# First input projection of a two-layer trunk: both conditioning products first, the filter's last layer behind the first tiles, the second token half normed in one piece

## The chip, the cores and the metric

One core of a Trainium2 chip. The metric is the device time of one execution in microseconds (us). Engines are named as in the profile: PE (TensorE matmul, PEld its weight loads), DVE (VectorE), ACT (ScalarE), POOL (GpSimd), SP (SyncE, which issues most loads). Each engine works through its own queue in order.

## The reference, cut to what matters

A two-layer trunk for 512 latent and 128 context tokens, width 1024. Layer 0 mixes an mLSTM and a Hyena long convolution behind one input projection, layer 1 is attention; each layer ends with a gated ConvFFN. What the change touches is the norm ahead of a sub-layer, its modulation from the conditioning vectors, and the filters of the long convolution:

```python
def adaln(cvec, w, b):
    mod = jax.nn.silu(cvec) @ w + b
    return jnp.split(mod[:, None, :], 6, axis=-1)
hp = rmsnorm(xp, g_mix[l]) * (1.0 + sc_p1) + sh_p1      # context
hs = rmsnorm(xs, g_mix[l]) * (1.0 + sc_s1) + sh_s1      # latents
proj = h @ w_in
# hyena_filters: two sine layers, then
filt = hdn @ w3
filt = filt * jnp.exp(-t * deltas)
# long_conv_bidir: K = rfft([h_past, 0, reversed h_future]); y = irfft(rfft(u) * K)
```

## The kernel before

The 640 tokens lie in the free dimension, features in the 128 partitions (8 blocks k of 1024). They are worked in two halves a of 320; the second half holds 192 latent and 128 context tokens, which have different shifts and scales. Every weight tile and activation is split in a high and a low fp32r part (`wh`, `wl`; `XH`, `XL`), and a product is three matmuls of 320 columns per k and half. `split_w` (L99 to L104) makes `wh` on ACT and `wl` on the engine it is given.

`norm_part` (L302 to L328) makes `XH` and `XL` of one k: for each range of tokens with one modulation a multiply on DVE (L321), a shift and cast on ACT (L325) and a subtraction on DVE (L326). The first half is one range, the second half two. One norm (`keep`, ahead of the last ConvFFN) has a form for the second half that takes the 320 tokens at once: a multiply by the row factor (L308), two scale-and-shift steps on ACT in place (L311), a cast on ACT (L313), a subtraction on DVE (L314). `norm_part` serves four norms: ahead of the input projection (n0), the first ConvFFN (n1), the attention (n2) and the last ConvFFN (n3, with `keep`).

`mixer_ab` (from L754) begins the program. In the order in which its instructions are written: the loads of the filter's tables and of x; the row factors of both halves (`rms`); the second step of the generator `hyena_filters` (the load of `w3`, the two sine layers on PE, ACT and DVE, sum and difference of `w3` on POOL, their split `wA` and `wB`, and five Exp steps `ad`); then `ada_pe` for feature half 0 (8 loads `wa` of 512 KB, 32 matmul records on PE, a copy `adasb` on ACT, 8 small matmuls `adaq`, then `mod` and `coefA` on DVE); the third filter step (20 matmuls `ff`, ten multiplies into `ad`, six steps for a boundary row on POOL); the norm of k 0 to 3; the first two projection tiles `hya0`, `hya1` with `wl` on POOL; `ada_pe` for half 1 with 8 more loads `wa`, which use the same 8 buffers again; the norm of k 4 to 7. Then `linear` runs the tiles `hya0` to `hya3`; the first two are a pair that takes k 0 to 3 of both halves and then k 4 to 7. After the pair the filter's last step follows (spectra: 28 matmul records `fa`, `fb`, `fp` of 512 columns, and DVE steps into `Ksp`, `Kpp`), then `hyena_chunk` and the tiles `hyb`.

PSUM has two pairs of banks (`pmt`) and four single banks (`pst`). Projection tiles and `ff` take pairs; `rms` holds two singles until the norm is done; `ada_pe` and the spectra take singles. A planner puts the instructions into each engine's queue: by and large as written, with later ones moved ahead where it reckons that the earlier ones must wait. So the queues of the trace are not strictly the written order.

Of the kernel before, what the change touches and what calls it, by code (L numbers as in the profile page):

```python
# [16 lines left out]
P = 128  # L17
# [5 lines left out]
HT = T // 2  # L23
# [13 lines left out]
def trunk(ctx: ExitStack, tc: tile.TileContext, I, O, dbg=None, stop=None):  # L37
# [19 lines left out]
    def pmt(nm):  # L57
        return psum["m"].tile([P, 2, 512], F32, tag="pm", name=nm)
# [40 lines left out]
    def split_w(raw, n, nm, eng):  # L99
        wh = wp.tile([P, 1024], F32R, tag="wh", name=f"{nm}h")  # L100
        wl = wp.tile([P, 1024], F32R, tag="wl", name=f"{nm}l")
        act.copy(out=wh[:, :n], in_=raw[:, :n])
        eng.tensor_tensor(out=wl[:, :n], in0=raw[:, :n], in1=wh[:, :n].bitcast(F32), op=ALU.subtract)  # L103
        return wh, wl  # L104

# [196 lines left out]
    def norm_part(l, which, nrm, a, rb, ks, keep=None):  # L302
        n = 2 * l + which
        for k in ks:
            if keep and a:
                t = keep[2 + k // 4][:, k % 4]
                c = slice(HT, T)
                dve.tensor_tensor(out=t, in0=x[:, k, c], in1=rb[:, :HT], op=ALU.mult)  # L308
                for c0, c1, s in RANGES[1]:
                    u = t[:, c0 - HT : c1 - HT]  # L310
                    act.activation(out=u, in_=u, func=AF.Identity, scale=coefA[:, n, k, s : s + 1],  # L311
                                   bias=mod[:, l, 3 * which, k, s : s + 1])
                act.copy(out=XH[:, k, c], in_=t)  # L313
                last = dve.tensor_tensor(out=XL[:, k, c], in0=t, in1=XH[:, k, c].bitcast(F32), op=ALU.subtract)  # L314
                continue
            for c0, c1, s in RANGES[a]:
                if keep:
                    t = keep[2 * a + k // 4][:, k % 4, c0 - a * HT : c1 - a * HT]
                else:
                    t = nrm.tile([P, HT], F32, tag="nt", name=f"nt{n}{k}_{c0}", bufs=4 if n == 0 else 6)[:, : c1 - c0]  # L320
                dve.scalar_tensor_tensor(out=t, in0=x[:, k, c0:c1], scalar=coefA[:, n, k, s : s + 1],  # L321
                                         in1=rb[:, c0 - a * HT : c1 - a * HT], op0=ALU.mult, op1=ALU.mult)
                b = mod[:, l, 3 * which, k, s : s + 1]
                oh, ol = XH[:, k, c0:c1], XL[:, k, c0:c1]
                act.activation(out=oh, in_=t, func=AF.Identity, bias=b)  # L325
                last = dve.scalar_tensor_tensor(out=ol, in0=t, scalar=b, in1=oh.bitcast(F32), op0=ALU.add,  # L326
                                                op1=ALU.subtract)
        return last.ins  # L328
# [320 lines left out]
    def hyena_filters(fl, spectra):  # L649
# [13 lines left out]
        for t_, n_ in ((z, "k_z"), (w1, "w_f1"), (fb, "f_cols"), (w2, "w_f2")):  # L663
            sp.dma_start(out=t_, in_=I[n_])
        yield
        w3 = load_raw(I["w_f3"], "fw3")
        for t_, n_ in ((delta, "k_delta"), (tneg, "k_tneg")):
            sp.dma_start(out=t_, in_=I[n_])

        ad = fl.tile([P, 2, 5, 512], F32, name="ad")  # L670
        frb = fl.tile([64, 2], F32, name="frb")
        for j in range(2):
            dve.tensor_tensor(out=frb[:, j : j + 1], in0=fb[:, 0:1], in1=fb[:, 1 + j : 2 + j], op=ALU.mult)
# [1 line left out]
        for j, w in enumerate((w1, w2)):  # L675
            pp = pmt(f"fm{j}")
            pt = [pp[:, 0], pp[:, 1]]
            pe.matmul(pt[0][0:64, :], w, hid[:, 0:512], start=True, stop=True)
            pe.matmul(pt[1][0:64, 0:128], w, hid[:, 512:640], start=True, stop=True)
            arg = arg_[j]  # L680
            for (c0, c1, a) in ((0, 512, 0), (512, 640, 1)):
                act.activation(out=arg[:, c0:c1], in_=pt[a][0:64, : c1 - c0], func=AF.Identity,
                               scale=fb[:, 0:1], bias=frb[:, j : j + 1])
            MAGIC = 12582912.0
            dve.tensor_scalar(out=kk, in0=arg, scalar1=1.0 / (2 * math.pi), scalar2=MAGIC, op0=ALU.mult, op1=ALU.add)
            dve.tensor_scalar(out=kk, in0=kk, scalar1=MAGIC, scalar2=None, op0=ALU.subtract)
            c1_ = 6.28125
            c2_ = float(np.float32(2 * math.pi - c1_))
            dve.scalar_tensor_tensor(out=arg, in0=kk, scalar=-c1_, in1=arg, op0=ALU.mult, op1=ALU.add)
            dve.scalar_tensor_tensor(out=arg, in0=kk, scalar=-c2_, in1=arg, op0=ALU.mult, op1=ALU.add)  # L690
            lim = 3.14159250
            dve.tensor_scalar(out=arg, in0=arg, scalar1=lim, scalar2=-lim, op0=ALU.min, op1=ALU.max)
            act.activation(out=hid[0:64, :], in_=arg, func=AF.Sin)
            if j == 0:

                for c, op in enumerate((ALU.add, ALU.subtract)):
                    pool.tensor_tensor(out=ws[:, c], in0=w3[:, 0:512], in1=w3[:, 512:], op=op)
                act.copy(out=wA, in_=ws)
                dve.tensor_tensor(out=wB[0:64], in0=ws[0:64], in1=wA[0:64].bitcast(F32), op=ALU.subtract)
                pool.memset(wB[64:].bitcast(F32), 0.0)  # L700

        hs = fl.tile([P, 640], F32R, tag="kk", name="hs", bufs=1)
        act.copy(out=hs[0:64], in_=hid[0:64])
        dve.tensor_tensor(out=hs[64:], in0=hid[0:64], in1=hs[0:64].bitcast(F32), op=ALU.subtract)
        for r in range(5):
            act.activation(out=ad[:, 0, r], in_=delta, func=AF.Exp, scale=tneg[:, r : r + 1])
        yield
        for r in range(5):
            pp = pmt(f"ff{r}")
            pt = [pp[:, 0], pp[:, 1]]  # L710
            lh = hs[:, r:512:4] if r < 4 else hs[:, 512:640]
            for j in range(2):
                pe.matmul(pt[j], lh, wA[:, j], start=True, stop=False)
                pe.matmul(pt[j], lh, wB[:, j], start=False, stop=True)
            for j in (1, 0):
                dve.tensor_tensor(out=ad[:, j, r], in0=pt[j], in1=ad[:, 0, r], op=ALU.mult)
            if r in (0, 4):

                row = fl.tile([64, 640], F32, tag="arg", name=f"row{r}", bufs=1)[0:1, 0:512]
                pool.tensor_tensor(out=row, in0=ad[0:1, 0, r], in1=ad[0:1, 1, r], op=ALU.add)  # L720
                for j in range(2):
                    pool.tensor_scalar(out=ad[0:1, j, r], in0=row, scalar1=0.5, scalar2=None, op0=ALU.mult)
        yield
        Ksp, Kpp, tabs = spectra
        for t_, n_ in ((tabs, "k_tabs"), (neg, "k_neg")):
# [28 lines left out]
    def mixer_ab():  # L754
        with ExitStack() as es:
# [29 lines left out]
            with ExitStack() as en:  # L785
                fl = en.enter_context(tc.tile_pool(name="fl", bufs=1, reuse_waits="tile"))
                nrm = en.enter_context(tc.tile_pool(name="nrm0", bufs=2, reuse_waits="tile"))
                sptr = []
                filt = hyena_filters(fl, sptr)
                es_a = en.enter_context(ExitStack())  # L790
                a0 = es_a.enter_context(tc.tile_pool(name="a0", bufs=1, side="right", reuse_waits="tile"))
                next(filt)
                for a in range(2):
                    c = slice(a * HT, (a + 1) * HT)
                    sp.dma_start(out=x[:, :, c], in_=I["x"][:, :, c])
                rbs = [rms(f"n0{a}", a, nrm) for a in range(2)]
                for t_, n_ in ((cwh, "w_conv_hy"), (cwq, "w_conv_qk")):
                    pool.dma_start(out=t_, in_=I[n_])
                next(filt)
                for half in range(2):  # L800
                    for _ in ada_pe(0, ((0, half), (1, half)), a0, "adr", 8):
                        pass
                    if half == 0:
                        next(filt)
                    for a in range(2):
                        norm_part(0, 0, nrm, a, rbs[a], range(4 * half, 4 * half + 4))
                    if half == 0:
                        pre = [load_w(w_, f"hya{j}", eng=pool) for j, w_ in enumerate(W(0, 1))]
                es_a.close()
                hy = es_h.enter_context(tc.tile_pool(name="hy", bufs=1, side="right", reuse_waits="tile"))  # L810
                tabs = hy.tile([P, 5, 2, P], F32, name="tabs")
                itab = hy.tile([P, 5, 2, P], F32, name="itab")
                Ksp = hy.tile([P, 4, 2, 4, P], F32, name="Ksp")
                Kpp = hy.tile([P, 4, 2, P], F32, name="Kpp")
                sptr.extend((Ksp, Kpp, tabs))
                linear(W(0, 1, 2, 3), done_h, "hya", filler=lambda: next(filt, 0), kcut=4, pre=pre, x_last=True)
                sp.dma_start(out=itab, in_=I["k_itab"])
# [819 lines left out]
```

## Time and profile before

| | |
|---|---|
| three runs | 1698.2, 1694.92, 1697.67 us |
| median | 1697.67 us |
| the profiled execution | 1698.56 us, span 1696.8 us |
| busy share of the span | PE 97%, DVE 69%, ACT 43%, POOL 8% |
| granted TensorE clock, mean | 0.993 of full speed |

The page gives busy times over the whole span. The change is made in the first 60 us and in three norms, so the stretches of the span have to be read one by one. A busy PE is not PE at its peak: matmul durations overlap, and a new matmul can start before the one before it is shown as ended. Start times tell the pace.

### The profile page before, as it was taken

The page shows a single profiled execution, that of the slowest core. Times are in us where ns is not written, and L with a number is a line of the kernel's source. Part 1 is how long each engine was busy: PE and PEld are TensorE (multiplying, and loading weights), DVE is VectorE, ACT ScalarE, POOL GpSimd, SP SyncE. Part 2 cuts the span into 40 slices and gives each one's busy share as a digit, 9 for nine tenths or more (in the row PEclk, how much of TensorE's full clock was granted, in tenths as well). Part 3 has the DMA queues.
Part 4 walks back from the last instruction along what each step waited for, and adds up shares of the span by engine and source line. Part 5 has one row for each costly group of instructions (what it writes and reads, how often), then busy time and mean ns, then how long its engine had stood idle before and what let it go on. Part 6 is the DMA issues. An engine that isn't in the chain of part 4 may idle for free. (4 is left out here: it accounts for less than half of the span.)

```text
span 1696.8 us, 28240 instructions
## 1 busy us (share of the span) xinstructions
PE 1642.3 (97%) x11206; PEld 1561.0 (92%) x11206; DVE 1179.1 (69%) x2361; ACT 735.2 (43%) x1380; POOL 135.0 (8%) x152
## 2 busy tenths in 40 slices
PE   5999999999999999999998999999999999999996
PEld 2699888999999999999998898889999999999996
DVE  5887556675887677777458555556388679587785
ACT  6333346663433123213336555656276335244353
POOL 3110001001000000000011212121010000000001
PEclk9999999999999999999999999999999999999998
DMA  8345422142364454454222211211224222222321
GB/s 332 109 125 173 162 75 69 53 142 75 98 179 150 146 157 148 145 181 139 66 77 98 69 57 61 62 48 42 63 61 112 75 82 87 82 75 72 91 81 69
DMA packets 59092, 177.60 MB, mean 105 GB/s; under 512 B 7808, under 2 KB 15792, under 8 KB 58704
## 3 DMA queue, kind: packets, MB, share of 16 engines
q1 hardware_dynamic: 57952, 173.66, 33.0%
q0 software_dynamic: 1008, 2.13, 0.7%
q8 instruction: 88, 1.44, 0.4%
q14 instruction: 44, 0.36, 0.1%
HBM read 169.61 MB, written 4.20 MB: 102 GB/s over the span
## 5 line engine op out<-in xcount | busy, mean ns | idle before, releaser
L350 DVE SCALAR_TENSOR_TENSOR x<-pd,mod,x 128x320 f32<-128x320 f32 (+2 forms) x168 | 64.1, 434 | 126.3 <-PE pd L127 120.4
L252 DVE CUSTOM_DVE_ANT_0 adj<-adw,cb 128x1024 f32<-128x1024 f32 x112 | 136.8, 1221 | 1.6
L372 DVE SCALAR_TENSOR_TENSOR fcb<-pu,cwf,fcb 128x384 f32<-128x384 f32 (+1 forms) x100 | 54.1, 549 | 1.9
L417 DVE TENSOR_TENSOR pr<-pu,ge 128x384 f32<-128x384 f32 (+1 forms) x42 | 18.8, 486 | 50.1 <-PE pu L127 49.2
L1334 DVE CUSTOM_DVE_ANT_0 s<-pS,bm 128x384 f32<-128x384 f32 x64 | 34.3, 553 | 26.7 <-PE pS L1333 26.0
L1236 DVE TENSOR_SCALAR s<-s,nm 128x384 f32<-128x384 f32 (+1 forms) x80 | 46.2, 584 | 1.7
L1234 ACT ACTIVATE s<-s,nm 128x384 f32<-128x384 f32 x64 | 39.1, 612 | 14.1 <-DVE nm L1334 12.3
L325 ACT ACTIVATE XH<-nt,mod 128x192 fp32r<-128x192 f32 (+1 forms) x72 | 29.7, 467 | 35.7 <-DVE nt L321 35.6
L1348 ACT COPY pTs<-pS 128x384 f32<-128x384 f32 (+1 forms) x80 | 33.8, 435 | 22.4 <-PE pS L1346 21.8
L1346 PE MATMUL pS<-ident,s 128*128 128x128 f32 x208 | 36.3, 281 | 5.5 <-DVE s L1236 5.5
L278 ACT ACTIVATE sqn<-x 128x320 f32<-128x320 f32 x56 | 25.3, 465 | 36.9 <-DVE x L350 32.9
L350 DVE SCALAR_TENSOR_TENSOR x<-pop,mod,x 128x320 f32<-128x320 f32 (+2 forms) x36 | 14.3, 433 | 36.6 <-PE pop L127 26.0
L103 POOL TENSOR_TENSOR qk00l<-qk,qk00h 128x1024 fp32r<-128x1024 f32 x1 | 2.8, 2766 | 461.6 <-DVE rn L293 461.6
L407 ACT ACTIVATE ge<-fcb 128x641 f32<-128x641 f32 x22 | 16.3, 742 | 52.0 <-DVE fcb L372 52.0
L1408 POOL TENSOR_TENSOR fo<-fo,rs 128x320 f32<-128x320 f32 x8 | 6.6, 858 | 395.7 <-ACT rs L1400 395.7
L326 DVE SCALAR_TENSOR_TENSOR XL<-nt,mod,XH 128x192 fp32r<-128x192 f32 (+1 forms) x72 | 35.0, 524 | 4.2 <-ACT XH L325 4.1
L615 DVE SCALAR_TENSOR_TENSOR fcb<-fca,cwf,fcb 128x641 f32<-128x641 f32 x38 | 33.6, 884 | 3.5 <-ACT fcb L613 3.2
L1308 POOL TENSOR_TENSOR bm<-amask,wr 128x768 f32<-128x768 f32 x14 | 25.7, 1838 | 117.6 <-issue 85.9
L1346 PEld LDWEIGHTS pS<-ident,s 128*128 128x128 f32 x208 | 23.5, 141 | 11.2 <-DVE s L1236 9.5
L279 DVE TENSOR_TENSOR accn<-accn,sqn 128x320 f32<-128x320 f32 x56 | 28.9, 522 | 7.0 <-ACT sqn L278 6.1
L127 PE MATMUL pd<-G,d_0h 128*128 128x320 f32 x176 | 33.2, 309 | 0.0
L127 PE MATMUL pd<-G,d_1h 128*128 128x320 f32 x176 | 33.1, 309 | 0.0
(2133 smaller groups left out, 5860.5 us busy)
## 6 DMA issues: line engine op xcount, KB each, us to landing
adw<-in_w_adaT SPq DMA_DIRECT2D x56, 512.0 KB, 3.7
u<-in_w_up SPq DMA_DIRECT2D x50, 512.0 KB, 3.6
wa<-in_w_ada SPq DMA_DIRECT2D x40, 512.0 KB, 5.0
qk<-in_w_qkv SPq DMA_DIRECT2D x24, 512.0 KB, 3.6
d<-in_w_down SPq DMA_DIRECT2D x16, 448.0 KB, 3.4
d<-in_w_down SPq DMA_DIRECT2D x16, 384.0 KB, 3.1
d<-in_w_down SPq DMA_DIRECT2D x16, 320.0 KB, 2.9
qk<-in_w_ab SPq DMA_DIRECT2D x8, 512.0 KB, 3.6
```

The lines of the kernel that those rows point to most:

```text
L127: pe.matmul(bank(pt, a)[:, : sp_[a][1] - sp_[a][0]], ww[:, kt], xx[:, slice(*sp_[a])], start=(first and n == 0), stop=(last and n == 2))
L252: dve.tensor_tensor_reduce(out=jk, in0=w, in1=cb[:, s], op0=ALU.mult, op1=ALU.add, scale=1.0, scalar=0.0, accum_out=acc[:, k, s : s + 1])
L325: act.activation(out=oh, in_=t, func=AF.Identity, bias=b)
L326: last = dve.scalar_tensor_tensor(out=ol, in0=t, scalar=b, in1=oh.bitcast(F32), op0=ALU.add, op1=ALU.subtract)
L350: r = dve.scalar_tensor_tensor(out=x[:, k, c0:c1], in0=bank(pt, h)[:, c0 - h * HT : c1 - h * HT], scalar=mod[:, l, ch, k, s : s + 1], in1= ...
L372: dve.scalar_tensor_tensor(out=o, in0=i, scalar=w[j], in1=o, op0=ALU.mult, op1=ALU.add)
L615: dve.scalar_tensor_tensor(out=o, in0=av[:, d : d + T + 1], scalar=w[j], in1=o, op0=ALU.mult, op1=ALU.add)
L1234: act.activation(out=s, in_=src, func=AF.Exp, scale=-1.0, bias=nm, accum_out=sm)
L1236: dve.tensor_scalar(out=s, in0=s, scalar1=sm, scalar2=None, op0=ALU.mult)
L1334: dve.tensor_tensor_reduce(out=s, in0=pS[:, 0:384], in1=bm[e][:, (0, 1, 1, 2)[i]], op0=ALU.add, op1=ALU.min, scale=1.0, scalar=3.0e38, acc ...
L1346: pe.transpose(pS[:, j * P : (j + 1) * P], s[:, j * P : (j + 1) * P], ident)
L1348: act.copy(out=t[:, : nk * P], in_=pS[:, : nk * P])
```

## The change

- `ada_pe` for both feature halves comes ahead of all norms; between them the first two projection tiles are loaded and split.
- For these two tiles `wl` is no longer subtracted on POOL: ACT writes minus `wh` into `wl`, and a DMA of POOL's queue adds the raw weights to it.
- The filter generator is cut in other places. Its second step ends with the sine layers. The load of `w3` and of the decay tables, sum and difference (now on DVE), `wA`, `wB`, the Exp steps and `ff` for r = 0, 1 come behind the first pair of tiles; `ff` for r = 2 to 4 behind the tile `hya2`; the spectra behind `hya3`. `ff` takes single banks. The boundary row is made on DVE.
- In `norm_part` the second half is normed at once in all norms, as it was with `keep`.

```diff
@@ split_w
+        if eng is None:
+            act.activation(out=wl[:, :n], in_=wh[:, :n].bitcast(F32), func=AF.Copy, scale=-1.0)
+            pool.dma_start(out=wl[:, :n], in_=raw[:, :n], accum_op=ALU.add)
+            return wh, wl
@@ norm_part
-            if keep and a:
-                t = keep[2 + k // 4][:, k % 4]
+            if a:
+                if keep:
+                    t = keep[2 + k // 4][:, k % 4]
+                else:
+                    t = nrm.tile([P, HT], F32, tag="nt", name=f"nt{n}{k}_w", bufs=4 if n == 0 else 6)
@@ hyena_filters
-        w3 = load_raw(I["w_f3"], "fw3")
...
-            if j == 0:
...
-                    pool.tensor_tensor(out=ws[:, c], in0=w3[:, 0:512], in1=w3[:, 512:], op=op)
...
         dve.tensor_tensor(out=hs[64:], in0=hid[0:64], in1=hs[0:64].bitcast(F32), op=ALU.subtract)
+        yield
+        w3 = load_raw(I["w_f3"], "fw3")
...
+        for c, op in enumerate((ALU.add, ALU.subtract)):
+            dve.tensor_tensor(out=ws[:, c], in0=w3[:, 0:512], in1=w3[:, 512:], op=op)
+        act.copy(out=wA, in_=ws)
+        dve.tensor_tensor(out=wB[0:64], in0=ws[0:64], in1=wA[0:64].bitcast(F32), op=ALU.subtract)
+        pool.memset(wB[64:].bitcast(F32), 0.0)
         for r in range(5):
             act.activation(out=ad[:, 0, r], in_=delta, func=AF.Exp, scale=tneg[:, r : r + 1])
-        yield
         for r in range(5):
-            pp = pmt(f"ff{r}")
-            pt = [pp[:, 0], pp[:, 1]]
+            if r == 2:
+                yield
+                yield
+            pt = [pst(f"ff{r}{j}") for j in range(2)]
...
-                pool.tensor_tensor(out=row, in0=ad[0:1, 0, r], in1=ad[0:1, 1, r], op=ALU.add)
+                dve.tensor_tensor(out=row, in0=ad[0:1, 0, r], in1=ad[0:1, 1, r], op=ALU.add)
@@ mixer_ab
-                for half in range(2):
+                def cond_half(half):
                     for _ in ada_pe(0, ((0, half), (1, half)), a0, "adr", 8):
                         pass
-                    if half == 0:
-                        next(filt)
+
+                cond_half(0)
+                pre = [load_w(w_, f"hya{j}", eng=None) for j, w_ in enumerate(W(0, 1))]
+                cond_half(1)
+                for half in range(2):
                     for a in range(2):
                         norm_part(0, 0, nrm, a, rbs[a], range(4 * half, 4 * half + 4))
-                    if half == 0:
-                        pre = [load_w(w_, f"hya{j}", eng=pool) for j, w_ in enumerate(W(0, 1))]
```

## Rows read from the trace of the kernel before

**Rows 1.** Stretches: from:to length, busy us (instructions) per engine, PE clock, DMA share, GB/s.
```profile
0.00:50.00 50.00, 31.30 (x118) 15.76 (x121) 28.79 (x62) 28.14 (x44) 17.18 (x28) 0.93 0.76 282
```
**Rows 2.** Timeline of SP's queue: start, duration, what is issued, how many.
```profile
4.74 2.10 SPq L96 DMA_DIRECT2D fw<-in_w_f  x1
...
7.93 8.30 SPq L220 DMA_DIRECT2D wa<-in_w_ada  x8
16.75 1.61 SPq L108 DMA_DIRECT2D hya<-in_w_ab  x2
28.05 5.68 SPq L220 DMA_DIRECT2D wa<-in_w_ada  x8
```
**Rows 3.** Stretches of 5 us, columns as in group 1.
```profile
20.00:25.00 5.00, 1.82 (x8) 1.65 (x8) 4.01 (x12) 4.97 (x9) 0.00 (x0) 1.00 1.03 410
25.00:30.00 5.00, 5.00 (x28) 1.95 (x27) 3.60 (x12) 4.91 (x7) 0.00 (x0) 1.00 0.53 197
...
35.00:40.00 5.00, 4.92 (x17) 4.02 (x18) 1.89 (x6) 2.77 (x4) 3.10 (x2) 0.61 1.02 415
```
**Rows 4.** Timeline of PE and DVE: start, duration, engine, line, out<-in, how many.
```profile
35.08 0.62 PE L713 MATMUL ff<-fwA,hs 128*128 128x512 f32 x1 [1.83 <-DVE hs L704]
...
48.78 0.41 PE L118 MATMUL phya<-XH,hya0h 128*128 128x320 f32 x1
...
54.10 1.06 PE L224 MATMUL ada<-wa,csil 128*32 128x512 f32 x6
...
58.42 0.16 DVE L208 SCALAR_TENSOR_TENSOR coefA<-mod,gains 128x8 f32<-128x8 f32 x1
...
93.47 0.63 PE L845 MATMUL ut<-ident,x 128*128 128x128 f32 x4
```
**Rows 5.** The stretch from the first tile to L845, columns as in group 1.
```profile
48.70:93.30 44.60, 44.60 (x245) 34.72 (x242) 36.71 (x81) 16.81 (x35) 4.34 (x3) 1.00 0.43 139
```
**Rows 6.** PE timeline, two pairs of spectra matmuls in a row.
```profile
73.38 1.02 PE L730 MATMUL fa<-ad,tabs 128*128 128x512 f32 x2
74.24 1.02 PE L731 MATMUL fa<-ad,tabs 128*128 128x512 f32 x2
```
**Rows 7.** Groups by shape: line, engine, operation, tile, count, busy us, mean ns.
```profile
L326 DVE SCALAR_TENSOR_TENSOR XL<-nt,mod,XH 128x192 fp32r<-128x192 f32 x24 | 10.0, 417 | 2.3 <-ACT XH L325 2.3
L321 DVE SCALAR_TENSOR_TENSOR nt<-x,coefA,rbn 128x192 f32<-128x192 f32 x24 | 9.8, 408 | 2.3 <-PE rbn L299 2.3
...
L326 DVE SCALAR_TENSOR_TENSOR XL<-nt,mod,XH 128x128 fp32r<-128x128 f32 x24 | 8.3, 345 | 1.6 <-ACT XH L325 1.6
L321 DVE SCALAR_TENSOR_TENSOR nt<-x,coefA,rbn 128x128 f32<-128x128 f32 x24 | 8.2, 341 | 0.0
```
**Rows 8.** Timeline, norm n3: the last step of two k in a row, second half.
```profile
1260.97 0.49 DVE L314 TENSOR_TENSOR XL<-keep,XH 128x320 fp32r<-128x320 f32 x1 [0.70 <-ACT XH L313]
...
1262.16 0.49 DVE L314 TENSOR_TENSOR XL<-keep,XH 128x320 fp32r<-128x320 f32 x1 [0.69 <-ACT XH L313]
```
**Rows 9.** PE's waits, 820 to 1000 us (n2): total us, times, longest.
```profile
PE pqk L121 <- DVE XL L326: 1.9, 3, 1.0
```
**Rows 10.** Timelines near 415 and 418 us: three L326 without and with POOL at work.
```profile
415.17 1.53 DVE L326 SCALAR_TENSOR_TENSOR XL<-nt,mod,XH 128x320 fp32r<-128x320 f32 x3
...
418.29 2.39 POOL L103 TENSOR_TENSOR u_2l<-u,u_2h 128x1024 fp32r<-128x1024 f32 x1 [2.86 <-ACT u_2h L102]
418.71 3.25 DVE L326 SCALAR_TENSOR_TENSOR XL<-nt,mod,XH 128x320 fp32r<-128x320 f32 x3 [0.30 <-ACT XH L325]
```
**Rows 11.** DMA issues: accumulating DMAs, count, KB each, us from issue to landing.
```profile
TT<-keep POOLq DMA_DIRECT2D x2, 640.0 KB, 5.6
```
**Rows 12.** Tile ff, its DVE step: count, ns min/median/max, first and last start.
```profile
L716 DVE TENSOR_TENSOR ad<-ff,ad x10: 681/688/693, 36.6 to 49.0; 128x512 f32<-128x512 f32 x10
```
**Rows 13.** Timeline, DVE: one weight split, the four steps of one conv3.
```profile
83.03 1.22 DVE L103 TENSOR_TENSOR hya3l<-hya,hya3h 128x1024 fp32r<-128x1024 f32 x1
...
88.56 2.31 DVE L372 SCALAR_TENSOR_TENSOR abc<-phya,cwh,abc 128x384 f32<-128x384 f32 x4
```

More of the change, by code (lines that the diff above doesn't have):

```diff
@@ L665, in hyena_filters @@
         yield
-        w3 = load_raw(I["w_f3"], "fw3")
-        for t_, n_ in ((delta, "k_delta"), (tneg, "k_tneg")):
-            sp.dma_start(out=t_, in_=I[n_])
-        ad = fl.tile([P, 2, 5, 512], F32, name="ad")
         frb = fl.tile([64, 2], F32, name="frb")
@@ L693, in hyena_filters @@
             act.activation(out=hid[0:64, :], in_=arg, func=AF.Sin)
-            if j == 0:
-                for c, op in enumerate((ALU.add, ALU.subtract)):
-                    pool.tensor_tensor(out=ws[:, c], in0=w3[:, 0:512], in1=w3[:, 512:], op=op)
-                act.copy(out=wA, in_=ws)
-                dve.tensor_tensor(out=wB[0:64], in0=ws[0:64], in1=wA[0:64].bitcast(F32), op=ALU.subtract)
-                pool.memset(wB[64:].bitcast(F32), 0.0)
         hs = fl.tile([P, 640], F32R, tag="kk", name="hs", bufs=1)
@@ L704, in hyena_filters @@
         dve.tensor_tensor(out=hs[64:], in0=hid[0:64], in1=hs[0:64].bitcast(F32), op=ALU.subtract)
+        yield
+        w3 = load_raw(I["w_f3"], "fw3")
+        for t_, n_ in ((delta, "k_delta"), (tneg, "k_tneg")):
+            sp.dma_start(out=t_, in_=I[n_])
+        ad = fl.tile([P, 2, 5, 512], F32, name="ad")
+        for c, op in enumerate((ALU.add, ALU.subtract)):
[3 more added lines that the diff above has]
+        pool.memset(wB[64:].bitcast(F32), 0.0)
         for r in range(5):
             act.activation(out=ad[:, 0, r], in_=delta, func=AF.Exp, scale=tneg[:, r : r + 1])
-        yield
         for r in range(5):
-            pp = pmt(f"ff{r}")
-            pt = [pp[:, 0], pp[:, 1]]
+            if r == 2:
+                yield
+                yield
+            pt = [pst(f"ff{r}{j}") for j in range(2)]
             lh = hs[:, r:512:4] if r < 4 else hs[:, 512:640]
@@ L719, in hyena_filters @@
                 row = fl.tile([64, 640], F32, tag="arg", name=f"row{r}", bufs=1)[0:1, 0:512]
-                pool.tensor_tensor(out=row, in0=ad[0:1, 0, r], in1=ad[0:1, 1, r], op=ALU.add)
+                dve.tensor_tensor(out=row, in0=ad[0:1, 0, r], in1=ad[0:1, 1, r], op=ALU.add)
                 for j in range(2):
-                    pool.tensor_scalar(out=ad[0:1, j, r], in0=row, scalar1=0.5, scalar2=None, op0=ALU.mult)
+                    dve.tensor_scalar(out=ad[0:1, j, r], in0=row, scalar1=0.5, scalar2=None, op0=ALU.mult)
         yield
```

## The prediction, made before the changed kernel ran

> **What bounds the kernel now.** I read the stretches of the span first. In the first 50 us PE is busy for 31.3 us [rows 1]; from 48.7 to 93.3 us it is busy in all 44.6 us [rows 5]. So TensorE is the bound from about 49 us on, and whatever it starts earlier there is worth its full length at the end, as long as the others keep up. Next the loads: from 20 to 25 us they run at 410 GB/s, from 25 to 30 us at 197, from 35 to 40 us at 415 [rows 3]. SP's queue shows why there is a hole: the second eight `wa` are issued from 28.05 us on [rows 2], since they use the buffers of the first eight. Then the order on PE: `ff` begins at 35.08 us, the first tile only at 48.78, and the last group of conditioning matmuls lies among the tiles at 54.10 [rows 4]. The granted clock is 0.61 of full speed from 35 to 40 us [rows 3], a mean over 1.2 and 2.4 GHz. `ff` holds the two PSUM pairs that the first tiles need, and each `ff` step waits for its DVE multiply; that, and `coefA` of half 1 at 58.42 [rows 4], is what the first tiles wait for.
>
> **The time of the conditioning products after the change.** `w3` and the decay table (0.77 MB) leave the queue ahead of `wa` [rows 2]: 0.77 / 0.41 = 1.9 us earlier. Before, eight `wa` (4.2 MB) at 0.41 MB per us from 28.05 us with an estimated 1.5 us until data flows again (the hole in [rows 3]) end at 39.8. Without `wB` (1.2 us, by width from [rows 13]) and without the DVE time that a POOL subtraction takes (1.7 us in [rows 10]) ahead of the row factors, PE reaches the first conditioning matmuls some 3 us earlier, so the hole of 25 to 30 us, worth 5 x (1 - 197/410) = 2.6 us, can close. That gives 35.3 us. Against it stand the two accumulating DMAs. One of 640 KB took 5.6 us [rows 11], so 512 KB take some 4.5; between nothing (they fall into a hole) and 5 us for both (all engines theirs) is added to the loads: 35.3 to 40.3 us. I take 38, the middle. The Trainium skill (DMA: Bandwidth & Descriptors, Issuing engines are not separate DMA queues) says that transfers started by any engine run on the same 16 DMA engines and interleave; this speaks against the change, and by it alone one would take the upper end, 40.3 us, and a gain 2.3 us smaller. The accumulating DMAs are issued on POOL, where nothing else is queued then. From the last conditioning matmul to `coefA` it took 58.58 - 54.10 = 4.5 us [rows 4]; with 0.3 us for that matmul to start, and 4 instead of 4.5 as DVE has less in line, `coefA` of half 1 stands at 42.3 us.
>
> **The norm.** In the first half a k costs two DVE steps of 0.51 us [rows 10], about 1.0. In the second half four DVE steps of 0.41, 0.34, 0.42, 0.35 us, together 1.51 [rows 7], become two; the form for all 320 tokens ran at one k in 1.19 us, paced by ACT's three steps [rows 8]. So k 4 to 7 need 4 x 1.0 + 4 x 1.19 = 8.8 us and end at 51.1. The norm of k 0 to 3 needs half 0 alone and is done by then. Ahead of its waits PE can run k 0 to 3 of the pair (48 matmuls), so the pair ends 0.4 us (only the last k left) to 3.5 us (all of k 4 to 7 of the second tile left) after the norm: 52.5 us.
>
> In n1 and n2 the same edit saves DVE 0.3 us or more per k, but no PE wait there hangs on the second half: the 1.9 us of n2 [rows 9] are waits in its first half, where DVE stands behind POOL. The pair or trio of tiles needs 9 matmuls per k, 1.3 us, longer than 1.19. ACT's extra step costs nothing as long as this cover holds; without it, 8 x 0.4 us at the worst in each norm. I take 0, with -1 and +2 as bounds for both.
>
> **TensorE up to L845.** Before, L845 starts at 93.47 [rows 4]. Spectra: two matmul records in 0.86 us [rows 6], 28 of them 12.0 us. The 44.6 us of [rows 5] less 12.0 and some 4 of conditioning leave 28.6 for 192 tile matmuls, 0.149 each. After the pair there remain `hya2` and `hya3` (96 matmuls, 14.3 us), the spectra (12.0) and `ff` (20 of 512 columns, by width 0.24 each, 4.8): 52.5 + 31.1 = 83.6 us, 9.9 us earlier than before. `ff` is only moved; its cover before was the wait for the loads.
>
> **What the gain runs into.** DVE gets work late that it did early or POOL did. After the norm it has, up to L845: three weight splits of 1.22 and three conv3 of 2.31 [rows 13], one product of 640 columns, 0.9 by width from [rows 12], ten `ad` steps of 0.69 [rows 12], `ws` and `wB` (2.6, by width from the same rows), the boundary row (six steps on one partition, never seen on DVE: 0.15 to 0.7 each by small steps and [rows 12]; I take 0.5, as they are short in partitions, not in columns) and 14 spectra steps of 0.68: 3.7 + 6.9 + 0.9 + 6.9 + 2.6 + 3.0 + 9.5 = 33.5 us, from 51.1 to 84.6. PE wants it by 83.6. So both engines are full for 32 us, with no slack between them. Not all of it will mesh: `ff` and the spectra share four single banks that DVE empties. I count 3 us of PE waits (1 from the two ends, up to 5 from the banks). What goes away with POOL helps: three DVE steps of 0.51 took 3.25 us together while POOL ran a subtraction [rows 10]. ACT moves five Exp steps of 512 columns and a table load behind the norm, an estimated 5 us with each step at the 0.69 of [rows 12], in a stretch where it was busy for 16.81 of 44.60 [rows 5], so they hide unless they are queued ahead of a norm step.
>
> The sum: 9.9 - 3 - 0 = 7 us. The profiled execution took 1698.56, so 1691.6 for one like it; the median of the runs is 0.9 lower, so I forecast **1690.7 us**.
>
> **The rivals.** Main case, 0.64: the sum, 1686 to 1694.5. (a) The second conditioning product stays late, 0.14: PE's queue again mixes tiles into it, or Exp steps wait for the decay table ahead of ACT's norm steps. Then `coefA` comes some 4 us later than I count and the gain is 3, 1694.5. For it speaks the mixture of [rows 4]; against it that the product is now written ahead of every tile. (b) DVE becomes the bound, 0.12: PE waits add up to 9 us instead of 3, 1696.7, no change. For it speak the 33.5 against 31.1 us; against it that the planner can move `hyb` tiles ahead. (c) Slower, 0.06: `ff` and spectra run as blocks with no tile matmul between. DVE then works 6.9 + 2.6 + 3.0 + 9.5 = 22 us in line with PE's 16.8, each of seven steps adds some 0.7 us of hand-over, and a conv3 and a split stand ahead (3.5): 22 - 16.8 + 4.9 + 3.5 = 13.6 us of waits, 3.7 more than the 9.9 gained, 1701.4 us. It decides from the point at which PE's waits between 52 and 95 us pass 9.9. (d) All meshes and the accumulating DMAs cost nothing, 0.04: 12.6 us gained, 1685.
>
> **How the numbers follow.** About 0.2% (3.4 us) is what a measurement of this kernel can tell from no change. Faster than 1694.3: nearly all of the main case, half of (a), (d): 0.73. Within: half of (a), (b), a little of the main case: 0.21. Slower: 0.06. The range reaches from the early end of the main case, with (d), to the far end of (b): 1685.5 to 1698.
>
> **What would show it.** Right: the eight later `wa` follow without a hole and the last conditioning matmul starts before 42 us; the first tile matmul starts by 40; `coefA` of half 1 at 40 to 45; L845 at 84 to 88; later stages unchanged, with no new PE wait at n1 and n2. Wrong: a PE wait on `hya0l` or `hya1l` of more than 3 us (the accumulating DMA), on `ad`, `ff` or `fa` of more than 3 us (DVE), or L845 after 92.

## The result and the profile after

The changed kernel takes 1717.84 us (median of 4 runs, 1716.82 to 1719.27) against 1697.74 us for the kernel before in the same session: ratio 1.0127, 95% interval 1.0113 to 1.0140. It is 20 us slower; the forecast was 7 us faster, and the time lies above the range. The span of the profiled execution is 1716.2 us, 19.4 more than before.

The first transpose of the convolution (L845 before, L854 after) tells where: 93.47 us before [rows 4], 112.23 us after, 18.8 us later. The stages behind it are shifted, not stretched: the tiles `pop` of the output projection start at 371.9 us before and 390.5 after. So the study is about the first 112 us.

Timeline of PE and DVE after (start, duration, engine, line, out<-in, count, idle time before and its releaser), columns as in [rows 4]:

```profile
35.99 0.64 PE L122 MATMUL phya<-XH,hya0h 128*128 128x320 f32 x1 [1.40 <-ACT XH L332]
...
44.33 0.64 PE L125 MATMUL phya<-XH,hya0l 128*128 128x320 f32 x1 [5.58 <-DMA hya0l<-hya]
...
58.66 1.06 PE L228 MATMUL ada<-wa,csil 128*32 128x512 f32 x6
...
61.78 0.17 DVE L212 SCALAR_TENSOR_TENSOR coefA<-mod,gains 128x8 f32<-128x8 f32 x1
...
71.91 0.85 PE L721 MATMUL ff<-fwA,hs 128*128 128x512 f32 x2 [0.20 <-ACT fwA L709]
...
79.60 0.53 PE L131 MATMUL phya<-XH,hya2h 128*128 128x320 f32 x2 [2.51 <-ACT hyb40h L102]
...
97.43 0.74 DVE L730 TENSOR_SCALAR ad<-row 1x512 f32<-1x512 f32 x2
...
99.04 1.02 PE L738 MATMUL fa<-ad,tabs 128*128 128x512 f32 x2
...
112.23 0.63 PE L854 MATMUL ut<-ident,x 128*128 128x128 f32 x4
```

The first tile matmul does start 13 us earlier. But the next one needs `hya0l`, and PE stands there for 5.58 us with 24 of the 32 matmul records of the second product behind it in its queue. The last group of conditioning matmuls comes at 58.66 us (54.10 before), `coefA` of half 1 at 61.78 (58.42 before). `ff` runs from 71.9 us on, in pieces up to 92 us; the spectra begin at 99.04 and end where the transpose starts.

Stretches of 5 us after (length, busy us and instructions of PE, PEld, DVE, ACT, POOL, PE clock, DMA share, GB/s), columns as in [rows 3]:

```profile
25.00:30.00 5.00, 5.00 (x28) 1.40 (x24) 2.43 (x8) 2.74 (x3) 0.00 (x0) 1.00 0.68 220
...
35.00:40.00 5.00, 2.76 (x8) 0.70 (x8) 4.95 (x11) 4.97 (x11) 1.63 (x2) 0.57 1.03 357
40.00:45.00 5.00, 0.67 (x2) 0.67 (x3) 1.96 (x5) 3.22 (x9) 0.00 (x0) 0.50 1.06 265
45.00:50.00 5.00, 5.00 (x15) 2.52 (x17) 0.00 (x0) 0.00 (x0) 0.00 (x0) 0.57 0.87 288
...
60.00:65.00 5.00, 3.29 (x20) 3.18 (x19) 3.42 (x10) 2.77 (x5) 0.00 (x0) 0.80 0.79 259
65.00:70.00 5.00, 4.96 (x29) 4.62 (x29) 4.53 (x10) 5.00 (x12) 0.00 (x0) 0.86 0.36 137
...
75.00:80.00 5.00, 2.49 (x10) 1.98 (x10) 5.00 (x11) 4.53 (x7) 0.00 (x0) 1.00 0.00 0
80.00:85.00 5.00, 4.13 (x14) 3.15 (x14) 5.00 (x10) 0.00 (x0) 0.00 (x0) 0.50 0.15 17
```

Three holes are new: one at 35 to 45 us, a short one behind 61 us, where the tiles wait for the norm that follows the late `coefA`, and one at 75 to 80. In or behind each of them the granted clock is below 1.00 (0.50 is all at the lower level, 1.2 GHz), so a hole costs twice.

The waits of PE from 30 to 113 us after (us in total, times, the longest):

```profile
PE phya L125 <- DMA hya0l<-hya: 5.6, 1, 5.6
PE phya L122 <- ACT XH L332: 3.1, 2, 1.7
PE phya L131 <- ACT hyb40h L102: 2.5, 1, 2.5
```

One row for the whole stretch from 30 us to the first transpose sums it up. Before:

```profile
30.00:93.47 63.47, 61.55 (x307) 43.48 (x305) 45.88 (x98) 25.76 (x48) 13.46 (x8) 0.95 0.50 172
```

After:

```profile
30.00:112.23 82.23, 69.17 (x310) 48.09 (x311) 48.82 (x95) 33.68 (x60) 1.77 (x2) 0.85 0.48 151
```

The stretch is 18.8 us longer. PE's idle time in it (length less busy) rises from 1.9 to 13.1 us, 11.1 of the 18.8. Its busy time rises from 61.6 to 69.2 us for about as many instructions (310 for 307), the other 7.6, while the mean clock falls from 0.95 to 0.85.

### The profile page after: what moved, and what is told of

The parts are those of the page before. It is cut to its first block, busy times and chain, and to the rows that moved or that the text cites. A ratio compares the mean times of both kernels' runs of the same rounds, so it can differ in the third digit from the quotient of the medians.

```text
span 1716.2 us, 28232 instructions
## 1 busy us (share of the span) xinstructions
PE 1651.2 (96%) x11206; PEld 1565.3 (91%) x11206; DVE 1171.6 (68%) x2321; ACT 745.0 (43%) x1403; POOL 120.2 (7%) x144
## 5 line engine op out<-in xcount | busy, mean ns | idle before, releaser
L131 PE MATMUL pd<-G,d_2h 128*128 128x320 f32 x176 | 32.9, 309 | 0.0
L131 PE MATMUL pd<-G,d_3h 128*128 128x320 f32 x176 | 32.9, 309 | 0.0
L131 PE MATMUL pd<-G,d_4h 128*128 128x320 f32 x176 | 32.9, 309 | 0.0
```

The lines of the kernel that those rows point to most:

```text
L131: pe.matmul(bank(pt, a)[:, : sp_[a][1] - sp_[a][0]], ww[:, kt], xx[:, slice(*sp_[a])], start=(first and n == 0), stop=(last and n == 2))
```

## The experiments

The expectations speak of three theories. **Q** blames the queues: tiles get mixed into the second product, and PE waits for `hya0l`. **F** blames the filter work that was moved late. **C** gives the reason: early on it lay in holes of TensorE, where it cost little. All runs in one table; "filter early" means cut as before, with the filter's third step between the two products. `coefA` is that of half 1, "transpose" the first one of the convolution, both from the one profiled execution, which lay up to 2.2 us off the median of its kernel.

| kernel | median us | ratio to before, 95% | coefA | transpose |
|---|---|---|---|---|
| changed | 1717.84 | 1.0127 (1.0113 to 1.0140) | 61.78 | 112.23 |
| edge: tiles behind the second product | 1709.97 | 1.0072 (1.0054 to 1.0090) | 50.16 | 104.96 |
| spool: `wl` on POOL | 1712.99 | 1.0089 (1.0074 to 1.0105) | 57.10 | 108.12 |
| edge_pool: both | 1707.33 | 1.0065 (1.0048 to 1.0082) | 48.02 | 101.69 |
| old_order: products as before | 1716.24 | 1.0120 (1.0105 to 1.0135) | 60.11 | 110.44 |
| norm_only: before, with the norm edit | 1696.81 | 0.9997 (0.9987 to 1.0006) | 58.59 | 92.11 |
| old_filter: changed, filter early | 1698.77 | 1.0008 (0.9998 to 1.0017) | 55.84 | 92.99 |
| of_edge: old_filter with edge | 1699.14 | 1.0011 (1.0002 to 1.0020) | 52.49 | 92.84 |
| of_edge_pool: also `wl` on POOL | 1698.63 | 1.0010 (1.0001 to 1.0019) | 52.35 | 92.69 |
| spec_late: `ff` early, spectra late | 1698.41 | 1.0014 (1.0005 to 1.0024) | 56.05 | 93.00 |
| ff_block: spectra right behind `ff` | 1716.98 | 1.0123 (1.0108 to 1.0138) | 61.51 | 110.86 |
| ff_single: before, `ff` on single banks | 1700.27 | 1.0022 (1.0012 to 1.0031) | 60.15 | 95.50 |
| nofilt_before: before, no `ff`, no spectra | 1693.45 | 0.9980 (0.9970 to 0.9989) | 56.76 | 87.99 |
| nofilt_after: changed, no `ff`, no spectra | 1699.29 | 1.0017 (1.0008 to 1.0026) | 62.54 | 94.92 |
| nospec_after: changed, no spectra | 1703.25 | 1.0042 (1.0027 to 1.0057) | 60.38 | 97.58 |

**Queue order.** `edge` puts every tile matmul behind the last conditioning matmul; `spool` makes `wl` of the first two tiles on POOL again; `old_order` undoes the new order of the products alone.

```diff
@@ edge
-                    pe.matmul(pt[32 * j : 32 * j + 32, :], csil[:, 2 * kp + par, :],
+                    psum["cond"] = pe.matmul(pt[32 * j : 32 * j + 32, :], csil[:, 2 * kp + par, :],
...
+                with tc.issue_after(psum["cond"].ins):
                   linear(W(0, 1, 2, 3), done_h, "hya", filler=lambda: next(filt, 0), kcut=4, pre=pre, x_last=True)
@@ spool
-                pre = [load_w(w_, f"hya{j}", eng=None) for j, w_ in enumerate(W(0, 1))]
+                pre = [load_w(w_, f"hya{j}", eng=pool) for j, w_ in enumerate(W(0, 1))]
@@ old_order
-                cond_half(1)
                 for half in range(2):
+                    if half:
+                        cond_half(1)
```

> The changed kernel with one ordering edge: no tile matmul enters TensorE's queue ahead of the last matmul of the second conditioning product. Theory Q (the queue order: tile matmuls mixed into the second product, and a tile matmul that waits 5.6 us for hya0l holds it up): the product ends by about 42 us instead of 59.7, some 16 us earlier, of which the tiles that then run later (48 matmuls, 7 us) come off; 1706 to 1709 us. Theory F (the filter work, moved late, is what costs): the stretch from the end of the second product to the first hyena transpose stays at 52 us or grows, and the total stays above 1713.

> The changed kernel with wl of the first two tiles subtracted on POOL again instead of by an accumulating DMA. Theory Q: the wait of 5.6 us for hya0l goes, and with it 5 to 6 us: about 1712. Theory F: no difference beyond 2 us, since the filter's work after the pair sets the end.

> The changed kernel, but the second conditioning product written behind the norm of k 0 to 3 again. If the new order of the products is itself a loss (tiles and second product mixed on TensorE, 5.6 us wait for hya0l), the time falls to 1712 us or less. If the planner mixes them either way, it stays at 1716 to 1719 us, coefA of half 1 at 61 to 62 us. If the new order is a gain, as predicted (7 us), it rises to 1722 us or more.

`edge` brings 7.9 us back (1 us less than Q expected, and more than F), `spool` 4.9 (near Q's figure), both together 10.5. They are not the same loss, nor do they quite add up; 10.8 us over the kernel before remain. `old_order` is level with the changed kernel (1.6 us apart): whichever way the products are written, the queue mixes them with tiles that wait for `hya0l`. In `edge` PE waits for the loads in place of `hya0l`:

```profile
PE ada L228 <- DMA wa<-in_w_ada: 4.1, 4, 2.0
```

So part of the 5.6 us at `hya0l` would have been waited for `wa` anyway; without the accumulating DMAs (`edge_pool`) PE waits 2.1 us for `wa`.

> The changed kernel with both repairs of its queue order: the tiles behind the last conditioning matmul on TensorE (alone 1710.0 us) and `wl` of the first two tiles on POOL (alone 1713.0 us). If the wait for hya0l and the mixing of tiles and second product are one and the same loss, this is the first run again, 1709 to 1711 us. If they add up, it is 1704 to 1706 us. Either way the rest over 1697 us is the filter work that came too late for its holes: 12 to 14 us under the first, 8 to 9 us under the second.

It falls between the two figures expected.

**The norm.** The norm edit alone, on the kernel before:

```diff
-            if keep and a:
-                t = keep[2 + k // 4][:, k % 4]
+            if a:
+                if keep:
+                    t = keep[2 + k // 4][:, k % 4]
+                else:
+                    t = nrm.tile([P, HT], F32, tag="nt", name=f"nt{n}{k}_w", bufs=4 if n == 0 else 6)
```

> The kernel before with the norm edit alone. All theories: within 2 us of before (1697.7), since no TensorE wait at the heads of the first ConvFFN and the attention hangs on the second half; if the loss sat in the norms it would show here as several us more.

Nothing that could be told from noise: the interval reaches from 0.13% faster to 0.06% slower.

**The filter put back.** Two kernels keep all of the change but the cut of the filter: `old_filter` has its early part and the spectra where they were; `spec_late` has `ff` early, but the spectra behind `hya3`.

```diff
@@ old_filter (and hyena_filters as before)
                 cond_half(0)
+                next(filt)
@@ spec_late (on top of old_filter)
         yield
+        yield
+        yield
+        yield
         Ksp, Kpp, tabs = spectra
```

> The changed kernel with the filter generator cut as before: w3, Exp steps and ff ahead of the tiles again, on the pairs, boundary row on POOL. Theory F: most of the 20 us go, 1698 to 1703. Theory Q: the wait for hya0l and the mixed queue stay, 1709 to 1716.

> The filter's last layer back at its early place as in the run with the filter cut as before, its spectra alone behind the tile hya3. This splits the 16 us that the late filter cost in two. If the cover of `ff` (the wait for loads and the second product, 35 to 48 us) is what was lost, this is the early-filter run again, 1698 to 1700 us, first hyena transpose at 93 to 94 us. If the spectra count as well, because in the kernel before they fill the holes between pair and hya2 (some 5 us, 69.9 to 74.9), it is 3 to 6 us over it, 1702 to 1705 us, transpose at 96 to 99 us.

`old_filter` takes away 19.1 of the 20 us, as F expected. `spec_late` is as fast: the late place in the written order does the spectra no harm, as long as `ff` is early. Its timeline of PE and POOL shows why:

```profile
34.96 0.63 PE L720 MATMUL ff<-fwA,hs 128*128 128x512 f32 x1 [0.74 <-DVE hs L711]
...
48.15 3.07 POOL L729 TENSOR_SCALAR ad<-row 1x512 f32<-1x512 f32 x2
...
59.22 1.02 PE L740 MATMUL fa<-ad,tabs 128*128 128x512 f32 x2
...
67.77 1.02 PE L741 MATMUL fa<-ad,tabs 128*128 128x512 f32 x2
...
72.06 1.02 PE L759 MATMUL fp<-ad,tabs 128*128 128x512 f32 x2
72.51 0.86 PE L131 MATMUL phya<-XH,hya2h 128*128 128x320 f32 x2
...
86.99 1.02 PE L740 MATMUL fa<-ad,tabs 128*128 128x512 f32 x2
...
93.00 0.63 PE L857 MATMUL ut<-ident,x 128*128 128x128 f32 x4
```

The planner moves seven pairs of spectra (6 us) ahead of `hya2`, into the time in which `hya2` can't start. It can, since the last step into `ad` has ended at 51 us. In the changed kernel `ad` is finished only at 98 us, behind `hya2`, and all 14 pairs stand between `hya3` and the transpose. And the clock, with `ff` in the wait for the loads:

```profile
35.00:40.00 5.00, 5.00 (x21) 3.87 (x22) 3.32 (x8) 5.00 (x7) 1.81 (x2) 1.00 1.01 406
40.00:45.00 5.00, 5.00 (x23) 2.30 (x25) 3.87 (x8) 0.59 (x2) 3.93 (x4) 1.00 0.97 324
45.00:50.00 5.00, 3.81 (x23) 1.53 (x16) 5.00 (x11) 2.65 (x6) 3.12 (x3) 1.00 0.77 152
...
30.00:93.00 63.00, 60.98 (x311) 42.53 (x306) 43.95 (x84) 33.66 (x60) 10.08 (x8) 1.00 0.57 180
```

PE is busy where the changed kernel has its first hole, and the clock stays at its higher level in the whole stretch.

Both kernels also bring back the pairs of banks for `ff` and the boundary row on POOL (its four steps take 2.8 us of DVE in the changed kernel). No run has the late filter with these put back alone, so their share of the 19.1 us is not shown.

**A better order on top of the early filter.** The same two repairs as above, where the filter is early:

> Filter cut as before, and the ordering edge that keeps the tiles behind the second conditioning product. Theory C (the filter's matmuls were what filled TensorE while loads, second product and norm went on; moved behind the pair they lose that cover): with the filler back and the product early, the first hyena transpose comes 3 to 6 us earlier than before (93.5), 1691 to 1694. Theory Q alone (queue order): the gain of the edge, 8 us as in the run of the edge alone, comes off 1698.8: about 1691. If neither product order nor edge matters once the filler is back: 1696 to 1699.

> As the run before it, with wl of the first two tiles subtracted on POOL. If the accumulating DMAs still cost (they compete with the loads of the second product and land late): 2 to 4 us less than the run before it. If POOL's subtractions and boundary row cost as much by holding DVE: equal.

`coefA` comes 5.9 us earlier than in the kernel before, the transpose 0.6 us, which is within what single executions differ by, and the time is 0.1% longer. This tells more of the premise than any other run: with the filter early, PE has 1.9 us of idle time left between 30 us and the transpose in the kernel before and 2.5 in `of_edge`, so an earlier `coefA` finds no idle time to take away. POOL in place of the DMAs changes nothing either.

**The price of the filter work.** `ff` and the spectra left out, with constants in `Ksp` and `Kpp`, before and after; and the spectra alone left out, after:

```diff
@@ nofilt_before, nofilt_after
-        w3 = load_raw(I["w_f3"], "fw3")
...
-            dve.tensor_copy(out=Kpp[:, :, cs], in_=c4(p3))
+        sp.dma_start(out=tabs, in_=I["k_tabs"])
+        pool.memset(Ksp, 0.01)
+        pool.memset(Kpp, 0.01)
@@ nospec_after
-        for cs in range(2):
-            src = ad[:, cs]
...
-            dve.tensor_copy(out=Kpp[:, :, cs], in_=c4(p3))
+        pool.memset(Ksp, 0.01)
+        pool.memset(Kpp, 0.01)
```

> The kernel before without the same filter work. Theory C: much of it lay in waits there, so leaving it out gives only 8 to 12 us: 1685 to 1689. Theory Q: the same 12 to 17 us as in the changed kernel: 1680 to 1685.

> The changed kernel without the filter's last layer and spectra (48 matmul records, their DVE, ACT and DMA work left out; constants stand in their place). Theory C: nothing covers that work in the changed kernel, so its whole 16.8 us on TensorE and the waits at its banks go: 1692 to 1697, 21 to 26 us less than the changed kernel. Theory Q: the waits for hya0l and for the late product stay and only some 12 to 17 us go: 1701 to 1706.

> The changed kernel with the spectra left out (28 matmul records of 0.43 us, 12.0 us of TensorE, and their DVE steps; Ksp and Kpp hold a constant), `ff` kept at its late place. Theory C, as the runs so far bend it: the spectra depend on `ad`, so with `ff` late the planner can't pull them into the holes before hya2, and they cost their full length; the time falls by 10 to 13 us, to 1705 to 1708 us, and what is left of the loss over the kernel without any filter work (1699.3) is `ff` with its chain, 5 to 8 us. The rival: spectra are as cheap late as in the run with early `ff` and late spectra (1698.4), and the whole loss is `ff`'s place on the queue; then the time falls by under 3 us, to 1715 us or more.

The filter work is 16.8 us of PE at the higher clock (20 matmuls at 0.24, 28 records at 0.43). Before, it costs 3.4 us, less than C and Q expected; after, 18.5 (1699.29 us lies between C's range and Q's). Of the 18.5 the spectra are 14.6, more than C expected, and `ff` the other 4.0, give or take 3 by the intervals of the two runs. The waits of the kernel before without it show the holes in which it lay:

```profile
PE phya L118 <- ACT XH L325: 5.2, 2, 3.5
PE phya L127 <- DVE abc L372: 4.9, 1, 4.9
PE adaq L232 <- ACT adasb L229: 1.5, 2, 0.8
```

Between the two kernels without filter work 5.8 us remain: that is what the rest of the change (order of the products, accumulating DMAs, norm) costs where there is no filter work. One can write the loss as 5.8 + 4.0 + 14.6 - 3.4 = 21.0 us, but that sum closes by its construction, each price being the distance to the next kernel. The prices depend on what lies beside them: with the filter early the rest of the change costs 2.0 us (`old_filter`; by its interval 0 to 3), and with the filter late the two repairs of the order bring back 10.5.

**Does the place behind the pair matter?** The filter as one block behind the pair:

```diff
-            if r == 2:
-                yield
-                yield
```

> The changed kernel, but the whole last layer of the filter in one piece behind the pair and the spectra right behind it, ahead of hya2; nothing between hya2, hya3 and the transposes. If what costs is that the filter's matmuls come after the holes in which they could hide, whatever their place behind the pair, it is within 3 us of the changed kernel, 1714 to 1720 us, less by the wait of hya2 (2.5 us) that the spectra can fill. If the place behind the pair is what costs (blocks without a tile between, waits for DVE), one block of 16 us is worse: over 1722 us, transpose after 116 us.

It is the changed kernel again. The spectra are now written ahead of `hya2`, but they still can't fill its wait (2.5 us, up to 79.35 us): PE starts them at 85.36 us, as DVE works on `ad` from 73.9 us on.

**Single banks.** The banks of `ff` alone, on the kernel before:

```diff
-            pp = pmt(f"ff{r}")
-            pt = [pp[:, 0], pp[:, 1]]
+            pt = [pst(f"ff{r}{j}") for j in range(2)]
```

> The kernel before with `ff` on single banks as in the change, all else as before. If the pairs of banks that `ff` held delayed the first tiles, these start earlier than 48.8 us and the time falls by up to 2 us (1694 to 1696). If the chain of second product, coefficients and norm sets the pace, the time stays, 1696 to 1698 us, and the first transpose stays at 93 us.

Neither: it is 3.9 us slower. The pairs did hold the first tile up. Freed of them it starts 8 us earlier:

```profile
40.62 0.63 PE L118 MATMUL phya<-XH,hya0h 128*128 128x320 f32 x1 [2.29 <-ACT XH L325]
...
60.15 0.17 DVE L208 SCALAR_TENSOR_TENSOR coefA<-mod,gains 128x8 f32<-128x8 f32 x1
```

But `coefA` of half 1 comes 1.7 us later. All 32 records of the second product stand in one block behind `ff` and the first tiles, where before they lay between 39.9 and 55.2 us:

```profile
54.08 3.64 PE L224 MATMUL ada<-wa,csil 128*32 128x512 f32 x32
```

That this place is what makes the kernel slower is my reading; no run tried it with the product put first.

## Why the prediction was wrong

**The premise.** "TensorE is the bound from about 49 us on, and whatever it starts earlier there is worth its full length": the first half was read rightly from [rows 5], the second does not follow from it. Between 30 us and the transpose PE had 1.9 us of idle time, and a mean clock of 0.95 over 61.6 busy us cost it an estimated 3 us. So another order of the same work could win some 5 us there; the sum counted 9.9. Nor was PE the only limit. `ff` and the spectra filled its holes; close under them lay a chain, second product, `coefA`, norm, conv3, `hya2`. `of_edge` pulls `coefA` 5.9 us earlier and gains nothing, `nofilt_before` takes 16.8 us of PE away and gains 3.4, `ff_single` starts the first tile 8 us earlier and loses 3.9 us.

**The second product: the term that failed most.** I put `coefA` of half 1 at 42.3 us; it came at 61.78. This is 19.5 of the 25.6 us by which the transpose missed (112.2, for 83.6 and 3 us of waits). The first half of the step held in part: `coefA` of half 0 came at 33.9 us, 5 earlier than before, and the eight later `wa` were issued from 25.95 us instead of 28.05 [rows 2], but the hole in the loads, counted as closed, hardly did (220 GB/s from 25 to 30 us, 197 before [rows 3]). Then rival (a) happened, and worse than I had priced it: not 4 us late, but 19.5. The mixture of [rows 4], which I took for a consequence of the written order, stays whatever is written (`old_order`). Even with the tiles kept out and `wl` on POOL, `coefA` comes at 48.0, so that 5.7 us of the estimate were wrong without any mixing. PE's rows of `edge_pool` split them:

```profile
40.64 1.06 PE L228 MATMUL ada<-wa,csil 128*32 128x512 f32 x6 [0.64 <-DMA wa<-in_w_ada]
...
45.84 1.87 PE L236 MATMUL adaq<-selc,adasb 128*128 128x4 f32 x8 [3.21 <-ACT adasb L233]
```

The loads let the last group start 2.3 us later than counted (38.3), and from there to `coefA` it took 7.4 us instead of 4: the copy `adasb` stands on ACT behind the norm of k 0 to 3, which the sum took as done by then, and starts at 45.20.

**The accumulating DMAs.** I gave 0 to 5 us for both. PE's wait for one was 5.6 us.

```profile
34.85 0.90 POOL L105 DMA_DIRECT2D hya0l<-hya  x1 [28.85 <-ACT hya0l L104]
```

Its issue at 34.85 us stood behind ACT, which makes `wh` and minus `wh` for it and began with them at 32.41, behind the copy `adasb`; then the transfer took 9.4 us beside the loads. "Nothing else is queued then" was true of POOL, and beside the point. For the loads the upper end of the price was the nearer one: from 20 to 60 us the two DMAs took 13.2% of the time of the 16 DMA engines, 5.3 us of all of them, and the 38 us that I took held 2.7.

**From `coefA` to the transpose.** I counted 41.3 us of work and 3 of waits; it was 50.45.

```profile
61.78:112.23 50.45, 45.40 (x200) 36.08 (x201) 40.72 (x74) 21.86 (x38) 0.00 (x0) 0.90 0.38 122
```

PE waits for 5.05 us in it, 2 more than I took. The mean clock is 0.90, an estimated 4.5 us more (a tenth of the 45.4 busy), which I had not in the sum at all. The filter work was there at its full 16.8 us, as I had put it.

**The cover of `ff`.** "`ff` is only moved; its cover before was the wait for the loads": the 4.8 us were in the sum, and `nospec_after` finds 4.0. What the sentence left out is what hangs on `ff`. With `ad` late the spectra can't move into the wait before `hya2`: they alone cost 14.6 us, where with early `ff` the whole filter work delays the transpose by 5.0 (93.00 in `spec_late`, 87.99 in `nofilt_before`). And with `ff` gone from there, PE stands idle for 6.6 of the 15 us from 35 to 50, and the clock is 0.50 to 0.57.

**Rivals.** (a) came true and was under-priced. (b): DVE was full from 75 to 85 us, but of the 3.4 us that PE waits there the profile puts 2.5 on ACT (`hyb40h`) and 0.9 on DVE; the 9 us did not come. (c) had the right side, and the blocks did form (the spectra all but alone from 99 to 112 us), but not for its reason: its point of decision was more than 9.9 us of PE waits between 52 and 95 us, and there were 5.3. The loss was in uncovered work, in the late `coefA` and in the clock.

**What held.** The norm edit is worth nothing, as taken. ACT's Exp steps did come ahead of norm steps (a table load at 63.60 us stands between two `XH`), the exception that I had named; the norm of k 4 to 7 took 11.5 us instead of 8.8. Later stages are unchanged. Of my own marks, the wait on `hya0l` over 3 us and the transpose after 92 both say "wrong", and point to the right place.

No complete kernel here beats the kernel before. `old_filter`, `spec_late` and `of_edge_pool` are level with it or 0.1% slower.

## What to carry to other kernels

A full engine is not yet the only bound: where a planner fills holes with side work, leave the side work out of both kernels once; if it costs 3.4 us of its 16.8, moving it can hardly win more than those 3.4. And before a gain is summed up, look how much idle time there is to take: here 1.9 us. Before work is moved behind something, ask what its result allowed to fill later holes (here `ad` and the spectra), not only what covered the work itself. And an in-order engine that gets a new reason to wait makes everything queued behind it late, so price the wait by what stands behind it.

## What was unexpected in the hardware

The same accumulating DMA of 512 KB (out<-in, queue, count, KB each, us to landing) takes very different times. In the changed kernel, beside the loads of `wa`:

```profile
hya0l<-hya POOLq DMA_DIRECT2D x1, 512.0 KB, 9.4
```

With the filter early, where it is issued behind them:

```profile
hya0l<-hya POOLq DMA_DIRECT2D x1, 512.0 KB, 4.2
```

My 4.5 us came from [rows 11], and beside the loads it was twice that. The Trainium skill (DMA: Bandwidth & Descriptors, Issuing engines are not separate DMA queues) says that DMAs started by any engine run on the same 16 DMA engines and interleave; the trace agrees with these two rows, 9.4 and 4.2 us. An accumulating DMA also takes longer than a load of its size: where the two run alone (44 to 48 us in `old_filter`) the DMA engines are full at 203 GB/s, where loads make 416 (36 to 40 us).

The other is the clock. From 35 to 50 us PE was idle for 6.6 us in the changed kernel and the granted clock 0.50 to 0.57; with `ff` in the same stretch (`spec_late`) 1.2 us idle and 1.00. In the kernel before it was 0.61 to 0.71 from 35 to 45 us, though PE was busy there: it had stood idle for 1.8 of the 5 us ahead of that, in `spec_late` for 0.7. The sum of the prediction had no term for it; of the 18.8 us it is up to 7.6. Executions differ in this: the mean clock of the span is 0.993 to 0.996 in those of the kernel before, 0.989 in the four of the changed kernel.
